# Conv tile 3 projected first, fewer of its taps on GpSimd, values ahead of scores: a hybrid decoder trunk on one core

## The chip, the core and the metric

The kernel runs on one core of a Trainium2 chip. The core has five engines, each with its own in-order queue of instructions: the tensor engine (PE in the profile), the vector engine (DVE), the scalar engine (ACT), GpSimd (POOL) and the sync engine (SP), which here only issues DMAs. They share a memory of 128 partitions; matmuls write to eight PSUM banks, which PE, DVE and ACT use and POOL does not in this kernel. The metric is the device time of one execution in microseconds (us), the median of the runs.

## What is computed

Two layers of a decoder trunk with 512 tokens and 1024 channels. Each layer is a gated feed-forward block, a mixer and another feed-forward block; the change lies in the mixer. Its reference, cut to what matters:

```python
h = rms_norm(x, mix_norm[l])
a, g, q, k, v = jnp.split(h @ w_in[l], splits, axis=-1)

u = a * sigmoid(g)                                   # conv group, 512 channels
y = depthwise_causal_conv(u, conv_w, 31 taps) + conv_b
conv_out = silu(rms_norm(y, conv_norm))              # norm over all 512 channels

q, k = rms_norm(q, q_norm[l]), rms_norm(k, k_norm[l])    # 4 heads, two maps of width 64 each
p = softmax(q @ k.T * scale + bias, causal)              # two maps per head
attn = p[:, :, 0] - lam * p[:, :, 1]
diff_out = rms_norm(attn @ v, subln_g) * (1 - lam_init)  # per head

x = x + concat([conv_out, diff_out]) @ w_out[l]
```

## The kernel before

Activations lie channel-major: a tile is 128 channels by 512 tokens. To keep fp32 accuracy at a higher rate, most matmuls are done in three parts (`mm3`, lines 158 to 164): weights and activations are each split into a rounded part `hi` and a remainder `lo`, and hi·hi, hi·lo and lo·hi are summed. A weight chunk of 128x1024 (`chunk`, line 100) takes a DMA on SP's queue into one of five slots `wraw`, an ACT copy to `whi` (line 97), and a subtraction to `wlo` (line 98) on DVE or POOL, whichever the caller names; there are four `whi` and four `wlo` slots. Scores, transposes and attention-times-values are plain f32 matmuls.

The mixer (from line 530) consists of these steps; the program's order is that of lines 777 to 800:

- `conv_in(c)`, for channel tiles 0 to 3: project a and g (48 matmuls of 512 columns), gate them, leave the padded tile `u`. Tiles 0 and 1 are done together. The weights of tile 3 are split on POOL, those of the others on DVE.
- `project(which, pair)`: keys (1) and queries (0) for two token tiles of 128 at a time, then their norm: squares on ACT, sums on DVE, a reciprocal root on POOL (`rsqrt`, line 209), the scaled result `qn` on DVE. `to_features` transposes it on PE (line 624), and ACT copies it out.
- `project_values(j)`: values of token tile j (24 matmuls, lines 615 to 617). The first call also loads and splits the four value chunks, on POOL.
- `conv_taps(c, n)`: the 31 taps of tile c. The first n are done by POOL and ACT: ACT multiplies the shifted tile by one tap (line 656), POOL adds the product (line 657). The others are done by DVE, one instruction each, accumulated in the one bank "y" (lines 664 to 670). Where both take part, line 673 adds the two sums. `POOL_TAPS` (line 50) gives n: all 31 of tile 0, none of tiles 1 and 2, 10 of tile 3. `conv_square` then adds the squares up on POOL (line 644).
- `attend(n)`: one step of a pipeline over 16 pairs of query tile and head, last query tile first: `softmaxes` (scores in a "sc" and a "po" bank, two exponentials on ACT, then the two maps joined by the scale c2, lines 713 to 717), two steps later `keys_first` (transposes), one step after that `values`, and a block's end two steps later (`block_out`).
- `conv_finish`: the row sums of the squares, their norm spread over all partitions, then for each tile a product on POOL (line 683), a tanh on ACT, and the two parts for the output projection (lines 686 to 688).
- the output projection (lines 804 to 814): first the conv half for all tokens (96 matmuls of 512 columns), in banks "sc" and "po" by turns, then the attention half.

Pairs of banks for `conv_in` and `project` go round "sc", "po", "mm" in the order of the calls (`turn`); values use "mm". The order in which each engine gets its instructions isn't quite that of the program: a planner (`schedule_with_timeline_sim`, line 916) sets it when the kernel is built, from its own estimates of durations, with the program's order as priority. Instructions that are ready may so move ahead of earlier ones.

Of the kernel before, what the change touches and what calls it, by code (L numbers as in the profile page):

```python
# [15 lines left out]
ALU = mybir.AluOpType  # L16
# [7 lines left out]
NT = SEQ // P  # L24
# [4 lines left out]
CT = CC // P  # L29
TAPS = 31  # L30
# [16 lines left out]

SPACE = 392

POOL_TAPS = (TAPS, 0, 0, 10)  # L50


_COLS = [
# [14 lines left out]
def trunk(ctx: ExitStack, tc: tile.TileContext, xt, par, lamv, relb, onehot,  # L68
          gu1, dn1, wag, wqkv, wout, gu2, dn2, out):
    nc = tc.nc  # L70
    V, S, G, T = nc.vector, nc.scalar, nc.gpsimd, nc.tensor
# [14 lines left out]
    def bank(tag, name):  # L86
        return psum.tile([P, 512], F32, tag=tag, name=name, bufs=BANKS[tag])
# [12 lines left out]
    def chunk(src, eng=None):  # L100
        raw, hi, lo = ring("wraw"), ring("whi"), ring("wlo")
        nc.sync.dma_start(raw, src)
        parts_of(raw, hi, lo, eng)
        return hi, lo
# [81 lines left out]
    for k0, k1 in ((0, 1), (1, 4), (4, KT)):  # L186
        h = slice(k0 * P, k1 * P)
# [83 lines left out]
    def wpart(w, b, n=P):  # L271
        return w[0][:, b * n : (b + 1) * n], w[1][:, b * n : (b + 1) * n]

    def products(pr, w, ps, i, at=None, amid=None):

        got = None
        for k in range(KT):
            if k == at:
                got = amid()
            mm3(ps, wpart(w[i], k), pr[k], k == 0, k == KT - 1, pin=at is not None and k in (0, at))  # L280
        return got
# [9 lines left out]
    def first_products(pr, w, ps, early=False):  # L291


        if not early:
            rc, v = rows_rstd(pr.s, DM)
            r = spread(rc, "rb", split=True)
        for k in range(KT):
            if early and k == STATS_AT:
                rc, v = rows_rstd(pr.s, DM, pin=True)
            for i in range(2):  # L300
                mm3(ps[0][i], wpart(w[0][i], k), pr[k], k == 0, k == KT - 1, pin=early and k in (0, STATS_AT))
        for i in range(2):
            for k in range(KT):
                if early and i == 0 and k == STATS_AT:
                    r = spread(rc, "rb", pin=True)
                mm3(ps[1][i], wpart(w[1][i], k), pr[k], k == 0, k == KT - 1, pin=early and k in (0, STATS_AT))
        return rc, v, r
# [4 lines left out]
    def pair_banks(turn):  # L312
        tag = turn_tag(turn)
        return [bank(tag, "ps_pair") for _ in range(2)]
# [179 lines left out]
    nlam, gq, gsub, ghalf = [], [], [], []  # L494
# [35 lines left out]
    def mixer(l, pr, after):  # L530
        with tc.tile_pool(name="mix", bufs=1) as mp, tc.tile_pool(name="mt", bufs=2) as mt:
# [5 lines left out]
            def conv_in(c):  # L537

                w = [chunk(wag[l, c, i], V if c < 3 else G) for i in range(2)]
                held.append((c, w, pair_banks(next(turn))))  # L540
                if c == 0:
                    return
                if c == 1:
                    row["c"], v, row["b"] = first_products(
                        pr, [h[1] for h in held], [h[2] for h in held], early=True
                    )

                    row["eps"] = small.tile([P, NT], F32, tag="rowe", name="rowe")
                    V.tensor_scalar(row["eps"], v, HD * EPS, None, op0=ALU.mult)

                    S.activation(small.tile([P, NT], F32, tag="rowx", name="rowx"), row["eps"], AF.Exp)
                else:
                    for i in range(2):
                        products(pr, w, held[-1][2][i], i)
                for n, _, ps in held:
                    gl = mt.tile([P, SEQ], F32, tag="gl", name="gl", bufs=1)
                    V.tensor_tensor(gl, ps[1], row["b"], op=ALU.mult)
                    S.activation(gl, gl, AF.Tanh, scale=0.5)
                    al = ps[0]
                    V.scalar_tensor_tensor(al, gl, 1.0, al, op0=ALU.add, op1=ALU.mult)  # L560
                    u = mp.tile([P, PAD + SEQ], F32, tag="u", name="u", bufs=4)
                    G.memset(u[:, :PAD], 0.0)
                    V.tensor_tensor(u[:, PAD:], al, row["b"], op=ALU.mult)
                    us[n] = u
                held.clear()
# [40 lines left out]
            def project_values(j):  # L606

                if 2 not in wts:
                    wts[2] = [chunk(wqkv[l, 2, kc], G) for kc in range(KT // 2)]
                t = slice(j * P, (j + 1) * P)  # L610
                ps = bank("mm", "ps_v")
                for k in range(KT):
                    wh, wl = wpart(wts[2][k // 2], k % 2, 512)
                    xh, xl = pr[k]
                    T.matmul(ps, xh[:, t], wh, start=k == 0, stop=False)
                    T.matmul(ps, xh[:, t], wl, start=False, stop=False)
                    T.matmul(ps, xl[:, t], wh, start=False, stop=k == KT - 1)  # L617
                S.activation(vv[:, j].rearrange("p h d -> p (h d)"), ps, AF.Copy, scale=row["c"][:, j : j + 1])

            def to_features(which, pair):  # L620
                for j in (2 * pair, 2 * pair + 1):
                    qn, pt = qns[which, j]
                    for h in range(HEADS):
                        T.transpose(pt[:, h * P : (h + 1) * P], qn[:, h * P : (h + 1) * P], ident)
                    pt = pt.rearrange("p (h t) -> p h t", h=HEADS)
                    t = slice(j * P, (j + 1) * P)
                    if which == 1:
                        S.activation(kt[:, :, t], pt, AF.Copy)
                    else:
                        for m in range(2):  # L630
                            S.activation(qz[:, m, :, t], pt, AF.Copy, scale=gq[l][:, m : m + 1])
# [62 lines left out]
            def softmaxes(i, h):  # L694
                W = (i + 1) * P
                tq = slice(i * P, W)
                if h == 0:
                    sums[i] = small.tile([P, 2, HEADS], F32, tag="sums", name="sums")
                scs = [bank(tag, "ps_sc")[:, :W] for tag in ("sc", "po")]
                e0 = mt.tile([P, SEQ], F32, tag="e0", name="e", bufs=4)[:, :W]  # L700
                sm = sums[i]
                for m in range(2):
                    T.matmul(scs[m], qz[:, m, h, tq], kt[:, h, :W], start=True, stop=True)  # L703

                for m, (sc, e) in enumerate(zip(scs, (e0, scs[1]))):
                    mn = small.tile([P, 1], F32, tag=f"mn{m}", name="mn")
                    V.tensor_tensor_reduce(
                        out=e, in0=sc, in1=row["bias"][:, h, SEQ - W :], scale=1.0, scalar=3e38,
                        op0=ALU.add, op1=ALU.min, accum_out=mn,
                    )  # L710
                    S.activation(e, e, AF.Exp, bias=mn, scale=-1.0, accum_out=sm[:, m, h : h + 1])

                r2 = small.tile([P, 1], F32, tag="r2", name="r2")
                V.reciprocal(r2, sm[:, 1, h : h + 1])
                c2 = small.tile([P, 1], F32, tag="c2", name="c2")
                V.tensor_scalar(c2, r2, nlam[l], sm[:, 0, h : h + 1], op0=ALU.mult, op1=ALU.mult)
                V.scalar_tensor_tensor(e0, scs[1], c2, e0, op0=ALU.mult, op1=ALU.add)
                maps[i, h] = e0

# [47 lines left out]
            def attend(n):  # L767
                if n < len(steps):
                    softmaxes(*steps[n])
                if 2 <= n < len(steps) + 2:  # L770
                    keys_first(*steps[n - 2])
                if 3 <= n < len(steps) + 3:
                    values(*steps[n - 3])
                if n >= 5 and steps[n - 5][1] == HEADS - 1:
                    block_out(steps[n - 5][0])

            for c in range(CT - 1):
                conv_in(c)
            project(1, 0)
            project(1, 1)  # L780
# [2 lines left out]
            to_features(1, 1)  # L783
            project(0, 1)
            to_features(0, 0)
            conv_in(CT - 1)
            to_features(0, 1)
            bias = mp.tile([P, HEADS, SEQ], F32, tag="bias", name="bias")
            nc.sync.dma_start(bias, skew[0])
            row["bias"] = bias  # L790

            for n in range(2):
                attend(n)
                project_values(NT - 1 - 2 * n)
                project_values(NT - 2 - 2 * n)
            for c in range(CT):
                conv_taps(c, POOL_TAPS[c])
            for n in range(2, len(steps) + 5):
# [122 lines left out]
```

## Time and profile before

| | us |
|---|---|
| runs: median of 3 (lowest, highest) | 1797.92 (1797.81, 1798.19) |
| the profiled execution | 1798.12 |
| its span, first to last instruction | 1796.4 |

Busy time over the span:

| engine | busy us | share |
|---|---|---|
| PE | 1785.4 | 99% |
| DVE | 1215.1 | 68% |
| ACT | 895.9 | 50% |
| POOL | 654.5 | 36% |

The first layer's mixer lies between about 358 and 565 us of the span, the second layer's 891 us later. In the lines of a profile, `L657 POOL TENSOR_TENSOR yp<-yp,prod` means line 657 of the kernel, on POOL, writing tile `yp` from `yp` and `prod`. A timeline line has the start and the length in us ahead of that, an xcount where several were merged, and in brackets the idle time before it with what ended it. In stretches, a pair of numbers such as "28.75 (x174)" is busy us and instructions of one engine. The granted clock of PE was 1.000 throughout.

### The profile page before, as it was taken

How to read it: one execution, taken by the hardware profiler on the slowest of the kernel's cores; microseconds unless marked ns; L12 is line 12 of the kernel's file. 1: busy time of each engine (PE TensorE's matmuls, PEld its weight loads, DVE VectorE, ACT ScalarE, POOL GpSimd, SP SyncE). 2: the span in 40 equal slices, each digit the busy share in tenths (PEclk: the TensorE clock that was granted, in tenths of full speed). 3: DMA queues.
4: the chain of work that ended last, by engine and by line, in shares of the span. 5: the costliest groups of instructions: out<-in, count | busy, mean ns of one | idle time of the engine just before them, and what ended most of it. 6: DMA issues, size and time to landing. Idle time of an engine off the chain costs nothing.

```text
span 1796.4 us, 28354 instructions
## 1 busy us (share of the span) xinstructions
PE 1785.4 (99%) x10845; PEld 1590.2 (89%) x10845; DVE 1215.1 (68%) x1862; ACT 895.9 (50%) x1482; POOL 654.5 (36%) x460
## 2 busy tenths in 40 slices
PE   9999999999999999999999999999999999999999
PEld 6899899888778899899888998998887888998997
DVE  7977477569867867477476764765788587673762
ACT  5555255445854446256433543654558354552651
POOL 4242232269843133132112312412797331322420
PEclk9999999999999999999999999999999999999999
DMA  7466476333212366466333664663231133664651
GB/s 242 104 167 197 100 178 187 107 105 94 71 48 83 94 164 179 115 170 184 110 94 95 171 169 115 179 182 118 71 113 52 48 106 89 168 178 112 178 151 59
DMA packets 111721, 231.24 MB, mean 129 GB/s; under 512 B 12151, under 2 KB 33414, under 8 KB 111584
## 3 DMA queue, kind: packets, MB, share of 16 engines
q1 hardware_dynamic: 91488, 191.93, 33.2%
q0 software_dynamic: 19808, 37.33, 12.7%
q8 instruction: 85, 1.39, 0.3%
q14 instruction: 52, 0.43, 0.1%
q10 hardware_dynamic: 288, 0.16, 0.0%
HBM read 227.26 MB, written 3.42 MB: 128 GB/s over the span
## 4 chain that ended last, share of the span: by engine, by line
PE 95%; DVE 2%; issue 1%; ACT 1%; ACTq 0%; DVEq 0%
PE ps_pair L373 38%; PE ps_d L160 9%; PE ps_d L164 9%; PE ps_d L163 9%; PE ps_pair L164 5%; PE ps_pair L163 5%; PE ps_pair L160 5%; PE ps_pair L585 2%; PE ps_pair L586 2%; PE ps_pair L587 2%; PE ps_out L163 1%; PE ps_out L160 1%; PE ps_sc L703 1%; PE ps_out L164 1%; DVE actl L258 1%; PE ps_v L617 1%
## 5 line engine op out<-in xcount | busy, mean ns | idle before, releaser
L97 ACT ACTIVATE whi<-wraw 128x512 fp32r<-128x512 f32 (+2 forms) x600 | 466.2, 801 | 616.4 <-PE ps_pair L373 225.7
L98 DVE TENSOR_TENSOR wlo<-wraw,whi 128x512 fp32r<-128x512 f32 (+2 forms) x556 | 527.4, 971 | 210.1 <-ACT whi L97 205.0
L373 PE MATMUL ps_pair<-acth,wlo 128*128 128x256 f32 x1088 | 307.9, 283 | 0.0
L373 PE MATMUL ps_pair<-actl,whi 128*128 128x256 f32 x1088 | 307.9, 283 | 0.0
L373 PE MATMUL ps_pair<-acth,whi 128*128 128x256 f32 x1088 | 307.9, 283 | 0.0
L163 PE MATMUL ps_d<-hl,whi 128*128 128x512 f32 x704 | 273.9, 389 | 0.0
L164 PE MATMUL ps_d<-hh,wlo 128*128 128x512 f32 x704 | 273.0, 389 | 0.0
L160 PE MATMUL ps_d<-hh,whi 128*128 128x512 f32 x704 | 268.4, 389 | 0.0
L373 PE MATMUL ps_pair<-th,wlo 128*128 128x256 f32 x816 | 230.9, 283 | 0.0
L373 PE MATMUL ps_pair<-tl,whi 128*128 128x256 f32 x816 | 230.8, 283 | 0.0
L373 PE MATMUL ps_pair<-th,whi 128*128 128x256 f32 x816 | 230.8, 283 | 0.0
L143 POOL TENSOR_TENSOR wraw<-wraw 128x512 f32<-128x512 f32 x68 | 104.1, 1531 | 345.5 <-DMA wraw<-in_gu 293.0
L138 POOL DMA_DIRECT2D wraw<-in_gu x68 | 82.0, 1206 | 384.1 <-DMA wraw<-in_gu 228.0
L373 PEld LDWEIGHTS ps_pair<-actl,whi 128*128 128x128 f32 x1088 | 208.9, 192 | 0.3
L373 PEld LDWEIGHTS ps_pair<-acth,whi 128*128 128x128 f32 x1088 | 208.9, 192 | 0.3
L373 PEld LDWEIGHTS ps_pair<-acth,wlo 128*128 128x128 f32 x1088 | 208.9, 192 | 0.0
L469 DVE SCALAR_TENSOR_TENSOR x<-ps_d,x 128x512 f32<-128x512 f32 x96 | 64.7, 688 | 179.1 <-PE ps_d L164 178.8
L164 PE MATMUL ps_pair<-acth,wlo 128*128 128x512 f32 x448 | 174.5, 391 | 1.1 <-DVE wlo L98 1.1
L163 PE MATMUL ps_pair<-actl,whi 128*128 128x512 f32 x448 | 174.6, 391 | 0.6 <-DVE actl L258 0.3
L160 PE MATMUL ps_pair<-acth,whi 128*128 128x512 f32 x448 | 174.5, 394 | 0.2
L373 PEld LDWEIGHTS ps_pair<-tl,whi 128*128 128x128 f32 x816 | 156.5, 192 | 0.7
L373 PEld LDWEIGHTS ps_pair<-th,whi 128*128 128x128 f32 x816 | 156.5, 192 | 0.6
(174 smaller groups left out, 3268.8 us busy)
## 6 DMA issues: line engine op xcount, KB each, us to landing
wraw<-in_gu SPq DMA_DIRECT2D x208, 256.0 KB, 4.0
wraw<-in_gu SPq DMA_DIRECT2D x104, 512.0 KB, 3.7
wraw<-in_gu POOLq DMA_DIRECT2D x68, 512.0 KB, 5.8
wraw<-in_wqkv SPq DMA_DIRECT2D x24, 512.0 KB, 3.6
wraw<-in_dn SPq DMA_DIRECT2D x84, 128.0 KB, 3.0
wraw<-in_dn SPq DMA_DIRECT2D x32, 256.0 KB, 3.1
wraw<-in_wag SPq DMA_DIRECT2D x16, 512.0 KB, 3.6
wraw<-in_wout SPq DMA_DIRECT2D x16, 512.0 KB, 3.6
```

Source lines behind the costliest of these rows:

```text
L97: S.activation(hi, raw, AF.Copy)
L98: (eng or V).tensor_tensor(out=lo, in0=raw, in1=f32(hi), op=ALU.subtract)
L138: nc.gpsimd.dma_start(two.rearrange("p (b c) -> p b c", b=2), u[:, h[0]].unsqueeze(1).broadcast_to([P, 2, 512]), accum_op=ALU.add)
L143: G.tensor_tensor(more[:, h[0]], two[:, h[1]], whole[:, h[0]], op=ALU.add)
L160: first = T.matmul(ps, wh, xh, start=start, stop=False)
L163: T.matmul(ps, wh, xl, start=False, stop=False)
L164: T.matmul(ps, wl, xh, start=False, stop=stop)
L373: mm = T.matmul(ps, l, r, start=first and i == j == 0, stop=False, skip_group_check=True)
L469: V.scalar_tensor_tensor(x[:, m, :], ps, 0.5, x[:, m, :], op0=ALU.mult, op1=ALU.add)
L585: T.matmul(ps[n], xh[:, t], wh, start=k == 0, stop=False)
L586: T.matmul(ps[n], xh[:, t], wl, start=False, stop=False)
L587: T.matmul(ps[n], xl[:, t], wh, start=False, stop=k == KT - 1)
```

## The change

Four edits. Six and not ten taps of conv tile 3 go to POOL and ACT. Tile 3 is projected right behind tiles 0 to 2, ahead of keys and queries. Values of the two last token tiles are projected ahead of the last query transposes and the first scores; those of the other two follow the first and the second step of attention. The scale c2 of the maps is written as a `scalar_tensor_tensor` and not as a `tensor_scalar` with two scalars from memory. (The load of the bias stays behind the first query transposes.)

```diff
-POOL_TAPS = (TAPS, 0, 0, 10)
+POOL_TAPS = (TAPS, 0, 0, 6)
...
                 c2 = small.tile([P, 1], F32, tag="c2", name="c2")
-                V.tensor_scalar(c2, r2, nlam[l], sm[:, 0, h : h + 1], op0=ALU.mult, op1=ALU.mult)
+                V.scalar_tensor_tensor(c2, r2, nlam[l], sm[:, 0, h : h + 1], op0=ALU.mult, op1=ALU.mult)
                 V.scalar_tensor_tensor(e0, scs[1], c2, e0, op0=ALU.mult, op1=ALU.add)
...
-            for c in range(CT - 1):
+            for c in range(CT):
                 conv_in(c)
             project(1, 0)
             project(1, 1)
...
             project(0, 1)
             to_features(0, 0)
-            conv_in(CT - 1)
-            to_features(0, 1)
             bias = mp.tile([P, HEADS, SEQ], F32, tag="bias", name="bias")
             nc.sync.dma_start(bias, skew[0])
             row["bias"] = bias
 
-            for n in range(2):
-                attend(n)
-                project_values(NT - 1 - 2 * n)
-                project_values(NT - 2 - 2 * n)
+            project_values(NT - 1)
+            project_values(NT - 2)
+            to_features(0, 1)
+            attend(0)
+            project_values(NT - 3)
+            attend(1)
+            project_values(NT - 4)
             for c in range(CT):
                 conv_taps(c, POOL_TAPS[c])
```

## The prediction

> **What bounds the kernel now.** I read the shares by engine first, then the chain of waits, then the busy times of the stretches round the changed code, and last the start times of single instructions. The page has the tensor engine (PE) busy for 1785.4 of 1796.4 us, and the chain agrees:
>
> ```profile
> PE 95%; DVE 2%; issue 1%; ACT 1%; ACTq 0%; DVEq 0%
> ```
>
> So only what PE loses can be won. The stretches of the first mixer say where that is (columns: stretch, length, then busy us and instructions of PE, PEld, DVE, ACT, POOL, clock, DMA):
>
> ```profile
> 376.00:488.00 112.00, 112.00 (x517) 90.26 (x516) 91.71 (x160) 72.48 (x121) 107.68 (x65) 1.00 0.29 85
> 485.00:516.00 31.00, 28.75 (x174) 22.97 (x173) 29.81 (x102) 24.31 (x73) 13.63 (x14) 1.00 0.04 16
> ```
>
> During the projections PE is never idle; POOL is nearly full (107.68 of 112 us), DVE is not (91.71). At the end of attention PE is idle for 2.25 us while DVE is full (29.81 of 31). The second layer shows the same 891 us later (2.24 us between 1376 and 1406). The worst wait:
>
> ```profile
> 501.97 0.38 PE L724 MATMUL ps_at<-ident,e 128*128 128x128 f32 x2
> 503.62 0.50 PE L160 MATMUL ps_out<-acth,whi 128*128 128x512 f32 x1 [1.26 <-ACT acth L687]
> ```
>
> PE has run out of attention and waits for the first conv channel tile before it may start the output projection. Followed back, that tile comes from `conv_finish`, which needs the sum of squares of all four conv tiles, and the last is tile 3:
>
> ```profile
> 483.65 2.62 POOL L657 TENSOR_TENSOR yp<-yp,prod 128x512 f32<-128x512 f32 x2
> 486.47 1.27 POOL L657 TENSOR_TENSOR yp<-yp,prod 128x512 f32<-128x512 f32 x1 [0.20 <-ACT prod L656]
> 489.95 1.27 POOL L644 TENSOR_TENSOR csum<-csum,csq 128x512 f32<-128x512 f32 x1 [2.21 <-ACT csq L643]
> ```
> ```profile
> 470.01 3.12 DVE L669 SCALAR_TENSOR_TENSOR ps_y<-u,par,ps_y 128x512 f32<-128x512 f32 x4
> 488.52 0.68 DVE L673 TENSOR_TENSOR u<-ps_y,yp 128x512 f32<-128x512 f32 x1
> ```
>
> DVE had its taps done at 473.13; POOL's share came at 487.74, and 15.9 us after that (503.62) PE gets its operand. POOL's share sets the conv chain.
>
> **How much PE loses.** Busy time hides waits, since each matmul's shown length is longer than its pitch. I took starts instead. In long runs a 128x512 matmul of the split operands starts every 0.227 us, and an f32 one every 0.11 us for each 128 columns. What starts later than that between 485 and 516 adds up to 5.1 us (5.0 in the second layer). About 1.3 us of it are steps of 0.06 to 0.13 us where PE changes between the two kinds; the rest, 3.8 us (second layer 4.0), are waits: 0.58 at 489, 0.36 at 494, 0.17 to 0.26 three times up to 500.5, 1.43 at 502, 0.21 to 0.32 three times behind it. The Trainium skill ("Perfetto Trace Analysis", Identifying the Most-Contended Engine) says that matmul busy time is a poor measure of headroom because matmuls are pipelined; the trace agrees, 2.25 us idle against 3.8 us lost. By idle time alone all that could be won in two layers would be 4.5 us, by starts 7.8 us.
>
> **The change, part by part.**
>
> *Taps of tile 3.* In each layer POOL loses 4 adds of 1.296 us (5.2 us), ACT loses 4 products of 0.717 us, and DVE gains 4 taps; dependent taps start 0.785 us apart (8 in 6.29), so 3.1 us. POOL's chain falls by 5.2 us at least; if the four adds that go are the last four (480.10, twice from 483.65, 486.47), with the weight splits between them, it ends at 475.5 and not 487.7, 12.2 us earlier. DVE's part, at 473.13 now, would go to 476.3.
>
> *Tile 3's projection ahead of keys and queries.* PE runs the same matmuls in another order: two times 24 of 0.227 us, 10.9 us, go from 436.7 to 391.4. Tile 3 can then be tapped from about 403 and not 452. That lets DVE use its idle time (9.4 of the 89 us from 384 to 473), which covers the 3.1 us added; without that cover DVE's part ends at 476.3, within a microsecond of POOL's earliest end, so it costs nothing. The DMAs move too: two wag loads of 512 KB pass eight wqkv loads in SP's queue, and the 1 MB bias load, already issued at 357.57, keeps its place ahead of the value weights. Landing takes 3.6 us and five raw slots are loaded ahead; I take 0, bounded by one landing, 3.6 us later, where the slots run dry, and 0 on the other side, as PE never waits for a load here. On POOL the two wag splits (2.41 us each) pass eight wqkv splits; key weights are then used 10.9 us later too, so their slack stays as it is (the fourth chunk is split by 395.9, and its twelve matmuls start 8.2 us after the first at 391.4).
>
> *Values ahead of scores.* Two tiles of values (24 matmuls, 5.45 us each) now cover the second query pair's norm where tile 3's projection did. In the trace the last query matmul starts at 436.47, and its normalised queries are there at 448.40, 11.9 us. The new cover is 10.9 us, and 0.8 us for the first pair's eight transposes: 11.7. I take 0; bounds: 0.8 us gained a layer (PE starts 0.4 us late at 460.5 and at 463.3, round the scores, and one or both may go) and 4.8 us lost (two value splits ahead of the norm on POOL).
>
> *The maps' scale.* A TENSOR_SCALAR with two pointer scalars (L716) takes 268 ns. A small op with immediates takes 154 (L740); a pointer scalar costs about 60 more, as the 128x512 rows show (694 without at L560, 754 with one at L669, 814 with two at L664). So the new form, with one pointer, should take about 211, and 16 maps save 0.9 us of DVE a layer. DVE is full there, but PE is to get other work, so I count 0.2 us a layer, between 0 and 0.9. The Trainium skill ("VectorE: DVE Perf Modes", The perf-mode tier table) lets an fp32 tensor_scalar run at twice the rate of a two-tensor op and so speaks against the swap; on one element a row there is nothing to stream, and by that rule alone this term would be 0, the total 0.4 us later.
>
> **The sum.** Tile 3 closes (L673) at 476 to 483 and not 488.5; I take 478.5, 10 us earlier. The steps from there (square, sum, row sums, norm, spread, tanh, 14.4 us) meet a fuller ACT and DVE, so I take the first output product at about 495. From 495 on the conv half of the output projection (96 matmuls of 0.227 us, 21.8 us) fills PE's gaps. Of the 3.3 us of waits from 494 on I credit two thirds, 2.2 us, less 0.3 us for three more changes of kind: 1.9 us a layer, between 0 (nothing comes earlier) and 3.3. Attention may end later without harm: its last block's transposes (L760 at 533.99) lie inside output products already. Two layers: 2 x (1.9 + 0.2) = 4.2 us. The profiled execution would go from a span of 1796.4 to 1792.2; it took 1798.12, 1.72 more than its span, and the runs' median is 0.2 lower, 1797.92. So about **1793.8 us**.
>
> **Rivals.**
>
> *Nothing gained.* Each engine's order is set by a planner when the kernel is built, and it may put the weight splits of the output projection (four of 2.4 us between 471.85 and 483.7) ahead of POOL's few adds. Tile 3 would then close 5.2 us earlier or less, the first output product would come at 499 or later, and only part of the 1.43 us wait would go. The banks speak for it too: output products need the "sc" and "po" banks, two each, that the scores hold. 0 to 0.9 us a layer: 1796.1 to 1797.9, say 1796.8. Against it: the splits were placed where POOL waited for ACT (0.18 at 471.85).
>
> *All gained.* If the products come by 490 and the scores find banks, the wait at 489 goes as well: 2 x (3.9 + 0.2) = 8.2 us, 1789.7. Attention's own latency speaks against it: most of the 0.2 to 0.4 us waits are between its steps.
>
> *Slower: the query norm loses its cover.* The cover of 11.7 us has no margin over the 11.9 us that the norm took. POOL is full there, and four value splits now fall due where two wag and two value splits did, at 2.4 us each, ahead of a 2.9 us rsqrt (L209 at 444.15, 3.6 us behind its input of 440.55). If two are queued before that rsqrt, the second pair's transposes come 4.8 us late, and PE, which runs in order, stands at L624; queued behind are the scores, the other values and so all of attention. 2 x 4.8 less 4.2 is 5.4 us slower: 1803.3. It decides from 2.1 us late in each layer on. Against it: two more value tiles (10.9 us) could be run first, and in the old order values did run ahead of these transposes (448.47 and 453.23).
>
> **Chances.** My forecast 0.50, nothing gained 0.17, all gained 0.11, slower 0.22. The forecast's own range is 1791.5 to 1795.0. Within 0.2% (3.6 us, about what a measurement of this kernel can tell from no change) lies what is above 1794.3. An eighth of the forecast (0.06) and the first rival make 0.23 for no change; 0.44 and 0.11 make 0.55 for faster; 0.22 for slower. The range goes from 1790.5, just above the second rival, to 1801.5, which leaves out about 0.13 of the third: **1790.5 to 1801.5**.
>
> **What would show it.** The add that combines tile 3 (L673) at 476 to 483; first output product (L160, ps_out) at about 495, without a wait over 1 us ahead of it; PE idle at the end of attention below 1 us a layer; the scale at about 211 ns; 70 adds at L657 and 168 taps at L669 in both layers, no longer 78 and 160. It is wrong if the wait for ACT L687 stays, or if PE waits ahead of L624, L615 or L585 in the projections, where it has no waits now.

## The result and the profile after

| | before | after |
|---|---|---|
| median of 4 runs each (lowest, highest), us | 1797.87 (1797.73, 1798.19) | 1813.66 (1811.44, 1815.89) |
| ratio to before (95% interval) | | 1.0088 (1.0075 to 1.0101) |
| the profiled execution, us | 1798.12 | 1811.44 |
| its span, us | 1796.4 | 1809.7 |
| its mean granted clock | 1.000 | 0.998 |

The change makes the kernel 15.8 us slower. Both layers pay: the first matmul of the next block's norm (L216) starts at 572.78 us in the first layer and not at 565.70, 7.1 us later, and the span grows by 13.3 us. The four runs of after differ by 4.5 us; their mean clocks of 0.998, 0.997, 0.997 and 0.996 go with 1811.44, 1813.35, 1813.98 and 1815.89 us. (The granted clock is the share of its full speed at which PE was let run.)

The chain of waits by engine, and the same two stretches of the first mixer (stretch, length, busy us and instructions of PE, PEld, DVE, ACT and POOL, clock, DMA):

```profile
PE 92%; DVE 4%; ACT 2%; issue 1%; POOL 0%; ACTq 0%; DVEq 0%; POOLq 0%
```
```profile
376.00:488.00 112.00, 110.03 (x495) 87.01 (x494) 96.03 (x154) 66.52 (x108) 103.79 (x62) 1.00 0.28 85
485.00:516.00 31.00, 26.99 (x155) 21.51 (x155) 28.06 (x93) 22.45 (x65) 9.14 (x10) 0.94 0.01 2
```

PE's share of the chain falls from 95% to 92%, DVE's doubles. In the first stretch PE was never idle and now is for 1.97 us; in the second its idle time grows from 2.25 to 4.01 us, and the clock, 1.00 before, is 0.94.

PE's timeline of after, from the first scores on (start, length, xcount where several were merged, idle time and what ended it):

```profile
471.00 7.12 PE L703 MATMUL ps_sc<-kt,qz 128*128 128x512 f32 x16
479.46 1.12 PE L703 MATMUL ps_sc<-kt,qz 128*128 128x512 f32 x2 [1.33 <-DVE e L717]
...
484.77 1.16 PE L733 MATMUL ps_o<-vv,at 128*128 128x128 f32 x8 [0.56 <-ACT at L726]
...
509.74 0.66 PE L760 MATMUL ps_o<-ident,ov 128*128 128x128 f32 x4 [1.35 <-DVE ov L748]
...
511.45 0.71 PE L733 MATMUL ps_o<-vv,at 128*128 128x128 f32 x4 [0.61 <-ACT at L726]
511.91 0.48 PE L160 MATMUL ps_out<-acth,whi 128*128 128x512 f32 x1
```

Three things stand here. The scores begin at 471.00 and not at 460.02. Two sets of scores in, PE waits 1.33 us for DVE. And the first output product comes at 511.91, 8.3 us later than before, although its operand was begun at 499.65 by ACT:

```profile
499.65 0.72 ACT L687 ACTIVATE acth<-yp,ghalf 128x512 fp32r<-128x512 f32 x1 [0.42 <-DVE yp L686]
```

DVE and POOL of after, round that wait of 1.33 us:

```profile
477.27 1.35 DVE L716 SCALAR_TENSOR_TENSOR c<-r,nlam,sums 128x1 f32<-128x1 f32 x1
478.65 0.75 DVE L717 SCALAR_TENSOR_TENSOR e<-ps_sc,c,e 128x512 f32<-128x512 f32 x1
...
480.54 1.61 DVE L740 SCALAR_TENSOR_TENSOR se<-sums 128x4 f32<-128x4 f32 x1
...
483.16 0.68 DVE L673 TENSOR_TENSOR u<-ps_y,yp 128x512 f32<-128x512 f32 x1
```
```profile
473.91 4.69 POOL L98 TENSOR_TENSOR wlo<-wraw,whi 128x1024 fp32r<-128x1024 f32 x2
478.54 1.28 POOL L657 TENSOR_TENSOR yp<-yp,prod 128x512 f32<-128x512 f32 x1
479.76 2.38 POOL L98 TENSOR_TENSOR wlo<-wraw,whi 128x1024 fp32r<-128x1024 f32 x1
485.31 1.28 POOL L644 TENSOR_TENSOR csum<-csum,csq 128x512 f32<-128x512 f32 x1 [3.17 <-ACT csq L643]
```

The scale L716, one element a row, takes 1.35 us and ends at 478.62; POOL's weight split ends at 478.60. L740, which no edit touches and which reads an SBUF tensor for both of its inputs, ends at 482.15, POOL's next split at 482.14. Between them L717 reads one operand from PSUM and one from SBUF, and keeps its 0.75 us although POOL works beside it. Tile 3 closes (L673) at 483.16, 5.4 us earlier than before.

### The profile page after: what moved, and what is told of

The parts are those of the page before. It is cut to its first block, busy times and chain, and to the rows that moved or that the text cites. A ratio compares the mean times of both kernels' runs of the same rounds, so it can differ in the third digit from the quotient of the medians.

```text
span 1809.7 us, 28339 instructions
## 1 busy us (share of the span) xinstructions
PE 1790.0 (99%) x10845; PEld 1592.5 (88%) x10845; DVE 1241.9 (69%) x1870; ACT 891.6 (49%) x1474; POOL 654.2 (36%) x452
## 3 DMA queue, kind: packets, MB, share of 16 engines
q8 instruction: 85, 1.39, 0.3%
## 4 chain that ended last, share of the span: by engine, by line
PE 92%; DVE 4%; ACT 2%; issue 1%; POOL 0%; ACTq 0%; DVEq 0%; POOLq 0%
PE ps_pair L373 38%; PE ps_d L160 9%; PE ps_d L163 9%; PE ps_d L164 9%; PE ps_pair L163 5%; PE ps_pair L164 5%; PE ps_pair L160 5%; PE ps_pair L587 2%; PE ps_pair L585 2%; PE ps_pair L586 2%; PE ps_out L160 1%; PE ps_out L164 1%; PE ps_out L163 1%; DVE actl L258 1%; PE ps_sc L703 1%
## 5 line engine op out<-in xcount | busy, mean ns | idle before, releaser
L98 DVE TENSOR_TENSOR wlo<-wraw,whi 128x512 fp32r<-128x512 f32 (+2 forms) x556 | 539.0, 991 | 194.3 <-ACT whi L97 187.9
L143 POOL TENSOR_TENSOR wraw<-wraw 128x512 f32<-128x512 f32 x68 | 113.9, 1676 | 357.2 <-DMA wraw<-in_gu 284.4
```

The source lines that it names most:

```text
L98: (eng or V).tensor_tensor(out=lo, in0=raw, in1=f32(hi), op=ALU.subtract)
L143: G.tensor_tensor(more[:, h[0]], two[:, h[1]], whole[:, h[0]], op=ALU.add)
```

## The experiments

Three suspects came out of this: the scale, held up by POOL; the new order, which starts attention 11 us later; and the taps, which change what DVE does during attention and how the output products stand in PE's queue. Each kernel is the one before with the edit named, unless it says otherwise; the runs of before beside them had medians of 1797.9 to 1798.1. First each part by itself.

**The scale alone.**

```diff
-                V.tensor_scalar(c2, r2, nlam[l], sm[:, 0, h : h + 1], op0=ALU.mult, op1=ALU.mult)
+                V.scalar_tensor_tensor(c2, r2, nlam[l], sm[:, 0, h : h + 1], op0=ALU.mult, op1=ALU.mult)
```

> The kernel before with the scale c2 as scalar_tensor_tensor and nothing else. Theory A (the new form reads two tensors from SBUF and can't finish while a two-input POOL instruction runs; in the changed kernel L716 and L740 take 3.3 us more per layer than L716 and L740 before, five of the 16 scales ending with a POOL instruction): slower by 2 to 8 us, 1800 to 1806, with L716 above 0.3 us wherever a POOL add or split overlaps it. Theory B (the new order starts attention 11 us later, with no values left to cover its waits; the scale is a bystander): within 1 us of 1797.9.

Measured: 1799.52 us, ratio 1.0008 (0.9999 to 1.0018). By the medians a loss of 1.5 us, not told from none. The groups of L716 in before and here (ns of the shortest, the median and the longest):

```profile
L716 DVE TENSOR_SCALAR c<-r,nlam,sums x32: 258/268/274, 466.3 to 1404.8; 128x1 f32<-128x1 f32 x32
```
```profile
L716 DVE SCALAR_TENSOR_TENSOR c<-r,nlam,sums x32: 200/220/1540, 466.2 to 1405.8; 128x1 f32<-128x1 f32 x32
```

The old form never took over 274 ns, whatever POOL did; the new one is shorter when nothing is in its way, and up to 1.54 us long.

**The whole change without the scale** (line 716 as before).

> The changed kernel with the old tensor_scalar for c2; order and taps as changed. Theory A: most of the 15.8 us come back, 1798 to 1801, and the granted clock is 1.000 again. Theory B: most of the loss stays, 1809 to 1813, with PE waits of over 1 us between 470 and 485 and a lower clock near 505.

Measured: 1806.36 us, ratio 1.0046 (1.0029 to 1.0063), clock 0.998 in the profiled execution. The scale on top of the other edits costs 7.3 us, five times what it cost alone. The wait behind the first scores is 0.26 us and not 1.33:

```profile
478.85 1.12 PE L703 MATMUL ps_sc<-kt,qz 128*128 128x512 f32 x2 [0.26 <-DVE e L717]
```

**The taps alone.**

```diff
-POOL_TAPS = (TAPS, 0, 0, 10)
+POOL_TAPS = (TAPS, 0, 0, 6)
```

> The kernel before with six POOL taps of tile 3 and nothing else. By the prediction's chain (POOL's share of tile 3 sets the conv chain, which PE waits for at 502): 1 to 4 us faster, 1794 to 1797. If the planner simply puts something else in POOL's place: within 1 us of 1797.9.

Measured: 1806.86 us, ratio 1.0050 (1.0035 to 1.0065): 8.9 us slower, the dearest part by itself. The conv chain came as early as the prediction had it, and yet PE's first product did not. DVE, ACT and PE of this run, and PE's stretch in it and in before:

```profile
478.74 0.69 DVE L673 TENSOR_TENSOR u<-ps_y,yp 128x512 f32<-128x512 f32 x1
```
```profile
497.47 0.71 ACT L687 ACTIVATE acth<-yp,ghalf 128x512 fp32r<-128x512 f32 x1
```
```profile
506.71 0.80 PE L703 MATMUL ps_sc<-kt,qz 128*128 128x128 f32 x2 [1.18 <-DVE e L717]
...
508.46 1.22 PE L733 MATMUL ps_o<-vv,at 128*128 128x128 f32 x4 [0.53 <-ACT at L726]
509.33 0.77 PE L160 MATMUL ps_out<-acth,whi 128*128 128x512 f32 x1
509.91 0.63 PE L163 MATMUL ps_out<-actl,whi 128*128 128x512 f32 x1
510.33 0.63 PE L164 MATMUL ps_out<-acth,wlo 128*128 128x512 f32 x1
```
```profile
500.00:510.00 10.00, 6.75 (x33) 4.89 (x32) 9.47 (x33) 8.06 (x24) 1.97 (x2) 0.82 0.01 2
```
```profile
500.00:510.00 10.00, 8.52 (x51) 6.44 (x49) 9.96 (x36) 9.37 (x30) 6.51 (x8) 1.00 0.01 2
```

The operand is there at 498.2, the product starts at 509.33, and in between PE waits again and again for attention's DVE and ACT, with work at hand that stands behind in its queue. PE is busy 6.75 of 10 us (before 8.52), the clock falls, and the first products start 0.42 us apart where 0.23 is the rule.

**The order alone** (the two hunks of the program's order in the change's diff).

> The kernel before with the new order (tile 3 ahead of keys, values ahead of scores), ten POOL taps, old scale. Theory A: within 2 us of 1797.9. Theory B: 1806 to 1813.

Measured: 1803.52 us, ratio 1.0031 (1.0019 to 1.0043), clock 1.000. The taps and the order each lose by themselves, 8.9 and 5.5 us, the scale perhaps 1.5. That they come near the whole 15.8 in sum is luck, since the pieces do not simply add (1806.36 for two of them, and not 1812.3). The scale alone, the change without it and the order alone all came out between the two ranges expected of them: none of the suspects explains the loss alone.

Next came the product's place. **An early output product** was tried with the taps, on before, and on after: `conv_finish` stands after step 12 of attention, and the first four output tiles of the conv half stand one each behind steps 14 to 17, in the bank "y" that the taps have left. `out_tile` holds what the body of the output loop did for one tile. The rest is as before.

```diff
+            early = 0
             for n in range(2, len(steps) + 5):
                 attend(n)
-            conv_finish()
+                if n == 12:
+                    conv_finish()
+                if n >= 14 and early < 4:
+                    out_tile(0, slice(0, SEQ), early, ('y',)[early % 1])
+                    early += 1
...
-                for m in range(KT):
+                for m in range(early if half == 0 else 0, KT):
...
-                    ps = bank(("sc", "po")[m % 2], "ps_out")[:, : t.stop - t.start]
+                    out_tile(half, t, m, ("sc", "po")[m % 2])
```

With the six taps:

> Six POOL taps alone, as in e3, and besides the conv end ahead of attention's step 13 in the program, and the first four tiles of the output projection's conv half behind steps 14 to 17, in the bank y, which the taps have left by then. Theory F (in e3 the conv operands were there at 498.2, 6 us earlier than before, but the first output product started at 509.3, because it needs a bank of the scores' two kinds and the planner gave those to attention; PE idles meanwhile and its clock falls to half): first product by 500, granted clock 1.000, 1794 to 1798. Theory D (the four added DVE taps and the earlier conv steps hold up attention on DVE, and the place of the products doesn't matter): 1804 to 1807, as e3.

On before:

> The kernel before with the same output products in bank y and nothing else: the control for e5. Theory F: the conv operands come at 503.6 as before, so at most the short waits behind that go: 1796 to 1798. Theory D: 1797 to 1799.

On after:

> The changed kernel with the output products of e5. Theory F: the waits from 497 on and the half clock go, and what the late start of attention and the stretched scales cost stays: 1802 to 1807, clock 1.000. Theory D: 1810 to 1816.

Measured: 1799.83 us with the taps, ratio 1.0009 (1.0000 to 1.0019); 1795.13 on before, 0.9983 (0.9974 to 0.9993); 1805.09 on after, 1.0039 (1.0025 to 1.0053). The clock is 1.000 in all three. With the taps, PE's first product and the stretch behind 500 are now:

```profile
498.57 0.48 PE L160 MATMUL ps_out<-acth,whi 128*128 128x512 f32 x1
```
```profile
500.00:510.00 10.00, 8.38 (x46) 5.89 (x45) 9.68 (x33) 8.31 (x24) 1.97 (x2) 1.00 0.01 2
```

The edit takes 7.0 us off the taps. It also wins 3.0 us on before (1798.10 beside it), faster than any range expected of it and than both kernels of this study, and 8.6 on after. So only about 4 of the taps' 8.9 us can be put down to the late products and the clock behind them: measured from 1795.13, the taps still cost 4.7 us.

**The taps and the scale, in the old order.**

> The changed kernel with the old order: six POOL taps and the new scale form. If the losses of e1 (1.5) and e3 (8.9) only add up: 1808 to 1809. If each loss lowers PE's activity and so brings the half clock on more often: 1809 to 1815, with a clock below 0.998.

Measured: 1810.21 us, ratio 1.0067 (1.0052 to 1.0082). That is more than the two losses in sum, and the clock is 0.998 to 0.996. On the taps the scale costs 3.4 us, on taps and order 7.3.

**The order, taken apart.** Tile 3 ahead of keys and queries, nothing else:

```diff
-            for c in range(CT - 1):
+            for c in range(CT):
                 conv_in(c)
...
-            conv_in(CT - 1)
```

> The kernel before with tile 3's projection ahead of keys and queries, and nothing else: values stay behind the steps of attention. Theory V (in e4 it is the values ahead of the scores that cost, since attention starts at 470 and not at 460 with no values left behind its first scores): within 1.5 us of 1798. Theory C (tile 3's projection was the cover of the second query pair's norm, and without it attention starts late whatever the values do): 1801 to 1806.

And the values ahead of the last transposes and the first scores, tile 3 where it was:

> The kernel before with the values' new order and nothing else: tile 3 stays behind the queries. Theory V: 1801 to 1806, with the scores starting at 468 or later. Theory C: within 1.5 us of 1798.

Measured: 1803.51 us for tile 3, ratio 1.0033 (1.0022 to 1.0045), and 1797.83 for the values, 1.0005 (0.9996 to 1.0015). The order's price is all tile 3's. With tile 3 early, PE and DVE:

```profile
464.22 1.03 PE L624 MATMUL ps_pair<-ident,qn 128*128 128x128 f32 x8
471.23 7.13 PE L703 MATMUL ps_sc<-kt,qz 128*128 128x512 f32 x16
...
482.94 0.59 PE L703 MATMUL ps_sc<-kt,qz 128*128 128x384 f32 x1 [0.53 <-DVE mn L707]
```
```profile
472.29 0.69 DVE L707 CUSTOM_DVE_ANT_0 e<-ps_sc,bias 128x512 f32<-128x512 f32 x1 [5.14 <-PE ps_sc L703]
```

With the values early:

```profile
459.93 3.59 PE L703 MATMUL ps_sc<-kt,qz 128*128 128x512 f32 x8
```

With tile 3 early the second pair's queries, and with them the scores, come 11 us later. All values have been projected by then: PE's first 16 matmuls of scores stand in one piece, DVE has sat idle for 5.14 us, and nothing is left to run between attention's first steps. In before and with the values early, values stand between the scores.

Something else differs, too. With tile 3 early, L740 is held up, though its form is the old one; it takes 0.16 us in before:

```profile
480.40 2.02 DVE L740 SCALAR_TENSOR_TENSOR se<-sums 128x4 f32<-128x4 f32 x1
```

PE's wait of 0.53 us at 482.94 is for the DVE instruction right behind it. With the order alone and with the taps alone L740 takes 2.02 and 1.76 us. So part of the price of both may go through this hold-up by POOL, and not through the values that are gone or the taps that were added; no run separates the two.

**Eight taps, with the early product.**

> e6 with eight POOL taps and not ten. If the conv operands' arrival is all that counts once the products have a bank: 1793 to 1795, faster than e6. If taps on DVE cost attention in proportion (e5 against e6: 4.7 us for four taps a layer): 1796 to 1798.

Measured: 1796.00 us, ratio 0.9987 (0.9978 to 0.9997): 0.9 us above the ten taps with the early product, whose interval it overlaps.

**The order, with the early product.**

> e6 with the new order and nothing else changed; it measures the order's cost where no half clock and no missing bank add to it. If the order costs by itself what e4 showed: 1799 to 1801. If it cost there mainly by leaving PE without filler at the end: 1795 to 1797.

Measured: 1799.96 us, ratio 1.0011 (1.0002 to 1.0021), 4.8 us above 1795.13: the early product does not mend the order.

**Bank or place in the program.** As the run with six taps and the early product, but in the scores' banks:

```diff
-                    out_tile(0, slice(0, SEQ), early, ('y',)[early % 1])
+                    out_tile(0, slice(0, SEQ), early, ('sc', 'po')[early % 2])
```

> Six taps alone; the norm of the conv group and four output tiles written earlier in the program as in the run with the bank of the taps, but in the scores' two kinds of bank, as before. If the bank was what held the products up (they wait for a bank that the scores hold): first output product (ps_out, L160) at 506 to 509.5 as with the six taps alone, half clock behind it, 1804.5 to 1807.5 us. If the place in the program was (PE's order put them behind the scores): first product at 497.5 to 500, clock 1.00, 1799 to 1801.5 us.

Measured: 1800.69 us, ratio 1.0015 (1.0006 to 1.0024), clock 1.000. The time is that of the place in the program; the first product is neither's, in PE's timeline:

```profile
503.60 0.49 PE L160 MATMUL ps_out<-acth,whi 128*128 128x512 f32 x1
```

Coming 5.7 us earlier than 509.33 is enough to keep the clock and 6.2 of the 7.0 us. The bank brought the product another 5.0 us forward and 0.9 us of time, which the intervals do not tell apart. The norm's and the products' place in the program were only tried together.

**The whole change without the scale, with the early product.**

> The whole change without the scale, with four output tiles in the bank of the taps. The scale cost 7.3 us where PE ran at half clock and 1.5 us by itself. If its own price is the 1.5 us, and the rest was the clock: 1803.6 us (1802.5 to 1804.5) against 1805.1 with the scale. If the swap costs as much wherever attention is late: about 1798 (1797 to 1799.5). Clock 1.00 in both.

Measured: 1799.57 us, ratio 1.0009 (1.0000 to 1.0019). The scale costs 5.5 us here (1805.09 less 1799.57), with the clock at 1.000 in both, so most of its 7.3 is its own and not the clock's; the 1.5 us that it costs alone was no guide. The wait behind the first scores is 0.26 us here, and 1.35 with the scale. From its first score to its second group of eight L733, PE takes 11.67 us here (470.79 to 482.46) and 13.78 with the scale (471.08 to 484.86), in the second layer 11.68 and 13.79, so this one place makes 2 x 2.1 = 4.2 of the 5.5 us. And this run is 0.4 us below that of the order with the early product: in the new order the four more taps of DVE cost nothing in sum. L740 takes 0.47 us here and 2.00 there, so the taps may cost something that this gains back.

## Why the prediction was wrong

The forecast was 1793.8 (its terms give 1793.7), its range to 1801.5; 1813.66 came. The sum had two gains a layer, 1.9 and 0.2 us, and three costs set to nothing. Step by step:

**Taps of tile 3** was right about the chain: by themselves they close tile 3 at 478.74 (taken: 478.5). The steps from there to the operand took longer than was taken, 19.4 us to 498.2 and not 16.5 to 495. In after it closed at 483.16, outside the predicted stretch by a hair, since the scale held DVE back (481.34 in the whole change without the scale). What was set at nothing, four more taps on DVE, depends on where they fall. In the new order they can run where DVE waits for the first scores, and in sum they cost nothing (1799.57 against 1799.96), as the prediction said, if not for its reason alone: L740 is shorter there by 1.5 us. In the old order the last of them fall between attention's steps, L740 is held up for 1.76 us behind them, and the two together cost 4.7 us with the early product.

**The sum** failed at its main term: "from 495 on the conv half fills PE's gaps". The operand was early and the product late, since PE takes its instructions in the order that the planner had fixed, and there the products stood behind attention's. The rival "nothing gained" named the planner and the banks, but priced them at no gain. With the taps alone the operand comes earlier and the first product 5.7 us later than before, at 509.33 and not 503.62. That is worse than nothing gained: the products that filled PE from 503.62 on no longer do. Of the 8.9 us of the six taps alone about 4 hang on this, as moving the products forward in both kernels showed, with the bank a minor part.

**The clock** is missing from the prediction altogether. Where it fell, it stood at half for 3.41 or 6.83 us and lost half of that: 1.7 us in each layer of after, 3.4 and 1.7 us with the taps alone, 3.4 in each layer with the taps and the scale, 3.4 in the second layer alone of after without the scale, and nothing in any trace with the early product. The Trainium skill ("TensorE: Matmul & The Clock Gate", HAM oscillation) has the clock at half after idle gaps of PE of more than about 3.4 us; the trace has half clock though the longest wait of PE in the 20 us ahead of it is 0.86 us in after and 1.18 with the taps alone. The traces do show a pattern. All changes of the clock in a trace lie whole multiples of 3.413 us apart. Cut along this grid, PE was busy for only 1.39 to 1.89 us in the stretch ahead of each of the seven drops (1.86 from 500.73 to 504.14 in after). In the other stretches of the sixteen traces, up to 1790 us, it was busy for 1.95 us or more, but for two of 1.89 and 1.93 right behind a drop.

**Tile 3's projection ahead** was set at 0, since PE would never stop and the loads and splits had their slack. PE does not stop there, indeed. But the forecast looked only at the stretch of the projections. The move puts attention's start 11 us later and uses up the values ahead of it, the only work that had filled PE between attention's first steps. The price is 5.6 us, paid after 471, not at L624; how much of it goes through the held-up L740 stays open. This is the rival "the query norm loses its cover", but through another door, so that its price (5.4 us) comes near is luck: two value splits did run on POOL just ahead of the root (448.90 to 453.67), yet the root lagged its input no more than before, and PE ran more values instead of waiting. The prediction counted "two more value tiles could be run first" against the rival; it was how the rival came true.

**Values ahead of scores**, set at 0, was right: -0.1 us.

**The maps' scale** was right in its size where nothing hinders it (about 211 ns forecast, 0.21 us seen at 484.91, where POOL is idle) and wrong in sign: the sixteen L716 take 6.2 us a layer in after, 4.3 in before. The old form has one tensor operand in SBUF and two scalars by pointer, the new one two tensors. The Trainium skill ("SBUF — State Buffer", Who interferes with whom) says that a DVE instruction with two SBUF inputs shares a read port with GpSimd, and whichever starts second waits until the other's whole instruction is over; the trace agrees, with ends 0.02 and 0.01 us apart at 478.6 and 482.1. This rule spoke against the swap, and the prediction weighed another in its place. In the old order, where values cover the first maps, the swap costs 1.5 us or nothing (3.4 with the taps), and 5.5 to 7.3 in the new one, where PE stands waiting for just this instruction.

Together: 5.6 us for the order (1803.5), 2.8 for the taps on top of it (1806.4), which is no more than the 3.4 that the clock lost in the profiled execution, and 7.3 for the scale (1813.7).

## What to carry to other kernels

Making an operand earlier wins nothing unless the instruction that uses it also stands earlier in its engine's queue; look at the queue's order, not only at what is ready. When independent work is moved ahead, ask which later latency it was covering, and what is left over for that. Before swapping a small instruction for a shorter one, compare where its operands lie: an op on one element a row was held up to 1.9 us by an instruction of another engine.

## What the runs showed of the hardware

- A DVE instruction with two tensor operands in SBUF waits for POOL's instruction on two tensors to end: the 0.21 us of L716 became up to 1.35 in after, 1.54 with the scale alone and 1.93 with the taps and the scale, while the form with one tensor and two pointer scalars took 0.26 to 0.28 us throughout. In the sixteen traces L716 and L740 take over 0.4 us 63 times, and each time they end 0.01 to 0.03 us behind an instruction of POOL.
- PE's clock fell to half with no wait of PE over 1.3 us in the 20 us ahead. In the traces it goes by stretches of 3.413 us on a fixed grid: each of the seven drops stands behind a stretch in which PE was busy for 1.89 us or less, as the profile counts it. So it matters how the waits fall on the grid. In the first layer of after without the scale PE is busy for only 6.66 of the 10 us from 500 on, but for 2.06 us or more in each stretch, and the clock stays. No run was made to test this. Executions of one kernel differ, too: one of ten with the values early took 1804.47 us at a mean clock of 0.998, though the traced one shows no drop.
